# One transformer layer on one core: unit 1's keys moved behind unit 0's scores, w_out's first half made in two steps, and the first pair's sums issued in the second pair

## The chip, the cores and the metric

The kernel runs on one core of a Trainium2 chip. Its time is the device time of one execution in microseconds (us). The engines of the core work side by side, each through its own list of instructions and in that list's order: TensorE (PE; its weight loads are shown as PEld), VectorE (DVE), ScalarE (ACT), GpSimd (POOL) and SyncE (SP), from which nearly all DMA transfers are issued. An instruction that waits holds up all that stands behind it on its engine.

## The reference

The reference computes one layer over 1024 latent tokens (a grid 64 wide) and 256 context tokens, model width 1024, all in fp32. Cut to what matters here:

```
h = modulate(rms_norm(x)); one projection gives q, k, v of two mixers A and B
o_a = windowed grouped-query attention      (8 heads of 64, context keys in the same softmax)
o_b = 2-D neighbourhood attention           (8 heads; 640 keys for 128 queries: 384 latent, 256 context)
x   = x + g1 * (concat(rms_norm(o_a), rms_norm(o_b)) @ w_out)      # 1024 x 1024
h2  = modulate(rms_norm(x))
out = x + g2 * ((silu(h2 @ w_gate) * (h2 @ w_up)) @ w_down)        # hidden width 2816
```

## The kernel before, in words

**Precision.** Products are made from fp32 operands split in two: `hi` is the operand rounded to a shorter format (a copy on ACT or a cast on DVE, L117 or L119), and `lo` is what is left (a subtraction on DVE or POOL, L120). A product is three matmuls: hi by hi, hi by lo, lo by hi. Line 120 is thus the line of very many instructions, and the tile's name tells which.

**Order.** The program is written in an order of its own, but the framework puts each engine's list in the order in which its own timeline has the instructions ready, with the written order as the tie's end. `tc.issue_after(ins)` asks that what is issued inside stands behind `ins` in that timeline. So moving a call in the source can move rows on every engine.

**Attention B and the output projection (about 430 to 700 us).** Mixer B is done in 16 units u = (C, hp_): C one of four column blocks, hp_ one of four pairs of heads. For a pair of heads `b_kv` loads the keys in four pieces (`kkb`, L557), transposes them on PE (L562) and copies them as fp32r into `KTb` (DVE L567, one piece in four by ACT L565). `b_q` does the like for queries (`qdb`, L574, L579; `QThb`, `QTlb`). `b_front` computes scores `s` into PSUM (L458, four for a unit), takes them with the bias `bt` off on DVE (`P`, `nm`, L620), puts them through the exponential on ACT (L622), and at the end takes the reciprocal of the sums (DVE L626) and scales four tiles `P` on POOL (L628). `b_back` transposes `P` (L642, copied to `PT` at L645 and L647), and multiplies with the values (L655 to L659). In the loop over u the front of one unit runs woven with the back of the unit before.

In the same loop the half of the output projection that takes mixer A's rows runs for u = 2 to 8 (`out_a`): `w_out`'s four tiles of 128 rows (`woraw`) are loaded in two halves each (L793, L794), scaled by a column on POOL (L799) and split into `wo`, hi on ACT, lo on POOL for the first and third tile and on DVE for the second and fourth (L120). All of this is `load_wo(0)`, called once at u = 1. `in_a` loads a block of mixer A's output (`oal`, L831), `out_proj` splits it on DVE (`oh` L119, `ol` L120) and multiplies (L823 to L825).

**FFN (about 700 to 1160 us).** The hidden width is done in 11 pairs jp of 256. For each pair `group(jp)` does the gate half and then the up half. Each half is a two-by-two block product made from seven products of sums (numbered 1 to 7), 12 matmuls each. Products 1, 5, 7 and 6 go to new banks of PSUM. Product 5 is copied out by ACT (`p5`, L1114), 7 and 6 are added on DVE to `p5` and `p1` (L1116, L1118). Then product 2 is accumulated onto bank 1, product 3 onto bank 5 and product 4 onto bank 7. For the first three pairs products 1 and 2 were made before. In the gate half DVE adds `p1` to the banks (`sg`, L1128, L1129), POOL adds the two (L1130), ACT takes SiLU (L1132). In the up half DVE adds (`uc`, L1141), POOL multiplies (L1137, L1138, L1142). The right operands are `B11`, `BT1`, `BT3`, `BT2`, `B22`, `BT4` for the products 1, 5, 7, 6, 3, 4. The weights of a half are loaded (`fraw`, L993), combined on POOL (`fs`, L980) and split into `fwhl` one half ahead. `f_combs(jp, gate)` then makes four sums of the pair's four gated tiles on DVE (`sc`, L1089 to L1092) for the third product (`w_down`), and three of the gated tiles and the four sums are stored to the array `f_d` in DRAM. From the third pair on pieces of a modulation (`gw`, L1053, DVE L1055) are put in between.

**w_down (about 1160 us to the end)** reads `f_d` back and multiplies, again in sums.

Of the kernel before, what the change touches and what calls it, by code (L numbers as in the profile page):

```python
# [43 lines left out]
US, UR = 13, 13  # L44
# [17 lines left out]
def block(tc, d, out, dbg=()):  # L62
# [386 lines left out]
    at = pool("at", bufs=2)  # L449

    def scores(segs, lh, ll):
        s = psA.tile([128, 1024], F32, name="s", tag="s", bufs=2)
        for n_, l in enumerate((lh, ll)):
            for o, rhs, n in segs:
                ov = s[:, o:o + n]
                if len(rhs.shape) == 3:
                    ov = ov.rearrange("p (r c) -> p r c", c=rhs.shape[2])
                T.matmul(ov, l, rhs, start=n_ == 0, stop=n_ == 1)  # L458
        return s
# [88 lines left out]

    kvs, vps = {}, {}

    def b_kv(hp_):
# [49 lines left out]
    def b_front(hp_, C, Ps, QT, bias):  # L601
# [4 lines left out]
        for R in range(2):  # L606
            r0 = 4 * R
            for h in range(2):
# [7 lines left out]
                else:  # L616
# [4 lines left out]
                                       3.0e38, ALU.add, ALU.min, nm[:, j:j + 1])  # L621
                S.activation(P, P, AF.Exp, scale=-1.0, bias=nm[:, j:j + 1],  # L622
                             accum_out=den[:, j:j + 1])
                Ps.append(P)
                yield
        V.reciprocal(den, den)  # L626
        for j in range(4):
            G.tensor_scalar(Ps[j], Ps[j], den[:, j:j + 1], 1.0, ALU.mult, ALU.mult)  # L628

# [93 lines left out]
    for u in range(16):  # L723
# [30 lines left out]
        if u == UR + 1:  # L754
            qtb[0] = b_q(0, 0)
            kin = {0: b_kin(0, 0)}
        if u == UR + 2:
            b_kv(1)
    qtb[1] = b_q(1, 0)
    PsB = []  # L760
    stores_done()
    run(b_front(0, 0, PsB, qtb[0], kin[0][0]), prev)
    o_rstd(0)
    at.release()
# [23 lines left out]
    def load_wo(grp):  # L788
        ws = []
        for c in range(4):  # L790
            raw = op.tile([128, D], F32, name="woraw", tag="xt", bufs=xtb[0])
            if grp == 0:
                load(raw[0:64], d["w_out"][c * 64:c * 64 + 64])  # L793
                load(raw[64:128], d["w_out"][256 + c * 64:256 + c * 64 + 64])  # L794
            else:
                load(raw, d["w_out"][512 + c * 128:512 + (c + 1) * 128])
            r = col[:, 64 + 4 * grp + c:65 + 4 * grp + c]
            if c in WOG:
                G.tensor_scalar(raw, raw, r, 1.0, ALU.mult, ALU.mult)  # L799
            else:  # L800
                V.tensor_scalar(raw, raw, r, None, ALU.mult)
            hl = wop.tile([128, 2, D], F32R, name="wo", bufs=4)
            split(hl[:, 0], hl[:, 1], raw, S, V if c % 2 else G)
            ws.append(hl)
        return ws
# [92 lines left out]
    for u in range(16):  # L898
# [16 lines left out]
        if 1 <= u < 9:  # L915
            if u == 1:
                wo = load_wo(0)
                nxt = in_a(0)
            else:
                out_a(u - 2, *nxt)  # L920
            if u == 8:
                out_a(7, *in_a(7))
                wo = load_wo(1)
        elif 9 <= u < 15:
# [160 lines left out]
    def f_combs(jp, gate):  # L1085
# [6 lines left out]
        V.tensor_tensor(s[3], a12, s[1], op=ALU.subtract)  # L1092
        return [(f_d[n - 1, jp], x) for n, x in
                ((1, a11), (2, a12), (4, a22), (5, s[0]), (6, s[1]), (7, s[2]), (3, s[3]))]

    def group(jp, early=None):
        gate = []
        for which, w in enumerate(FW):
# [4 lines left out]
            for n in (1, 5, 7, 6):  # L1103
# [13 lines left out]
                else:  # L1117
                    V.tensor_tensor(p1, pb[6], p1, op=ALU.add)  # L1118
            u2, v = p1, p5
# [14 lines left out]
            else:  # L1134
# [4 lines left out]
                for n, o in ((5, 1), (7, 2)):  # L1139
                    c = ev("uc")  # L1140
                    V.tensor_tensor(c, pb[n], u2, op=ALU.add)  # L1141
                    last[0] = G.tensor_tensor(gate[o], c, gate[o], op=ALU.mult)  # L1142
        return f_combs(jp, gate)[1 if early else 0:]

# [77 lines left out]

    ops1 = operands(1)
    for jp in range(NJ // 2):
        made = group(jp, early[jp] if jp < NA else None)
        if jp == NJ // 2 - 1:
# [187 lines left out]
```

## Time and profile before

| | |
|---|---|
| median of 3 runs | 1366.87 us (1366.67 to 1369.6) |
| profiled execution | 1369.69 us, its span 1367.6 us |
| mean granted TensorE clock | 0.987 |
| PE | 1299.4 us busy, 95% of the span |
| DVE | 920.5 us, 67% |
| ACT | 595.3 us, 44% |
| POOL | 620.0 us, 45% |

Times in the profile are us from the span's start. A row of a timeline gives start, length, engine, line of the kernel, operation, what is written and read, and in brackets the idle time of that engine just before it with the event that ended it. The granted clock is given as a share of full speed: 1.00 is 2.4 GHz, 0.50 is 1.2 GHz.

### The profile page before, as it was taken

The page shows a single profiled execution, that of the slowest core. Times are in us where ns is not written, and L with a number is a line of the kernel's source. Part 1 is how long each engine was busy: PE and PEld are TensorE (multiplying, and loading weights), DVE is VectorE, ACT ScalarE, POOL GpSimd, SP SyncE. Part 2 cuts the span into 40 slices and gives each one's busy share as a digit, 9 for nine tenths or more (in the row PEclk, how much of TensorE's full clock was granted, in tenths as well). Part 3 has the DMA queues.
Part 4 walks back from the last instruction along what each step waited for, and adds up shares of the span by engine and source line. Part 5 has one row for each costly group of instructions (what it writes and reads, how often), then busy time and mean ns, then how long its engine had stood idle before and what let it go on. Part 6 is the DMA issues. An engine that isn't in the chain of part 4 may idle for free. (4 is left out here: it accounts for less than half of the span.)

```text
span 1367.6 us, 18930 instructions
## 1 busy us (share of the span) xinstructions
PE 1299.4 (95%) x6537; PEld 1014.9 (74%) x6537; DVE 920.5 (67%) x1536; ACT 595.3 (44%) x1201; POOL 620.0 (45%) x537
## 2 busy tenths in 40 slices
PE   6998998999998799999979989999999999999997
PEld 4677886767666577777757768887887887888886
DVE  5687775577546564566567788757868776858662
ACT  5555424554455544455555423333332333654430
POOL 1477665342113444575414777677687663000000
PEclk9999999999999999999999999999999999999999
DMA  9445374265227766555273344455565554985732
GB/s 349 156 145 195 101 192 101 65 197 185 93 87 233 220 211 205 183 192 178 95 215 95 98 155 157 167 189 185 186 233 177 190 185 165 393 296 212 258 101 61
DMA packets 149571, 242.85 MB, mean 178 GB/s; under 512 B 43932, under 2 KB 66660, under 8 KB 149348
## 3 DMA queue, kind: packets, MB, share of 16 engines
q1 hardware_dynamic: 149476, 241.65, 53.8%
q8 instruction: 51, 0.84, 0.3%
q14 instruction: 44, 0.36, 0.1%
HBM read 177.91 MB, written 63.70 MB: 177 GB/s over the span
## 5 line engine op out<-in xcount | busy, mean ns | idle before, releaser
L1241 PE MATMUL pf<-dhl 128*128 128x512 f32 x588 | 134.9, 389 | 0.0
L256 PE MATMUL pg<-whi,hl 128*128 128x512 f32 (+1 forms) x368 | 133.0, 375 | 0.5 <-POOL hl L120 0.5
L254 PE MATMUL pg<-whi,hTh 128*128 128x512 f32 (+1 forms) x320 | 122.3, 382 | 7.5 <-ACT qc L329 5.7
L1241 PEld LDWEIGHTS pf<-dhl 128*128 128x128 f32 x588 | 110.4, 188 | 22.9
L255 PE MATMUL pg<-wlo,hTh 128*128 128x512 f32 (+1 forms) x320 | 120.8, 377 | 0.0
L120 DVE TENSOR_TENSOR fwhl<-fs,fwhl 128x512 fp32r<-128x512 f32 x88 | 96.6, 1106 | 31.1 <-ACT fwhl L117 15.5
L500 POOL TENSOR_SCALAR P<-P,den 128x640 f32<-128x640 f32 (+1 forms) x64 | 51.8, 828 | 118.4 <-DVE den L498 84.0
L980 POOL TENSOR_TENSOR fs<-fraw 128x512 f32<-128x512 f32 x44 | 62.9, 1436 | 85.7 <-DMA fraw<-in_w_up_dram 52.1
L256 PEld LDWEIGHTS pg<-whi,hl 128*128 128x128 f32 x368 | 70.5, 192 | 12.3 <-issue 0.8
L1241 PE MATMUL pf<-fdhl 128*128 128x512 f32 x336 | 78.4, 390 | 0.5 <-DVE fdhl L120 0.4
L120 DVE TENSOR_TENSOR dhl<-draw,dhl 128x512 fp32r<-128x512 f32 x98 | 62.6, 686 | 24.1 <-ACT dhl L117 24.1
L117 ACT ACTIVATE dhl<-draw 128x512 fp32r<-128x512 f32 x98 | 55.8, 624 | 51.3 <-PE pf L1241 42.5
L254 PEld LDWEIGHTS pg<-whi,hTh 128*128 128x128 f32 x320 | 61.6, 192 | 20.3 <-ACT qc L329 7.2
L117 ACT ACTIVATE fwhl<-fs 128x512 fp32r<-128x512 f32 x88 | 54.8, 627 | 48.9 <-PE pf L1019 41.6
L1241 PEld LDWEIGHTS pf<-fdhl 128*128 128x128 f32 x336 | 62.9, 188 | 14.4 <-DVE fdhl L120 1.4
L117 ACT ACTIVATE fwhl<-fraw 128x512 fp32r<-128x512 f32 x54 | 34.0, 630 | 80.8 <-PE pf L1019 72.8
L490 ACT ACTIVATE P<-P,nm 128x640 f32<-128x640 f32 (+1 forms) x64 | 51.0, 798 | 40.3 <-DVE nm L488 40.2
L255 PEld LDWEIGHTS pg<-wlo,hTh 128*128 128x128 f32 x320 | 61.8, 193 | 8.8
L120 DVE TENSOR_TENSOR fwhl<-fraw,fwhl 128x512 fp32r<-128x512 f32 x54 | 68.2, 1262 | 0.1
L628 POOL TENSOR_SCALAR P<-P,den 128x640 f32<-128x640 f32 x64 | 50.8, 815 | 34.8 <-DVE den L626 28.2
L488 DVE CUSTOM_DVE_ANT_0 P<-s,mska,nsink 128x640 f32<-128x640 f32 (+1 forms) x64 | 52.4, 846 | 18.1 <-PE s L458 15.9
L622 ACT ACTIVATE P<-P,nm 128x640 f32<-128x640 f32 x64 | 52.7, 824 | 16.4 <-DVE nm L620 16.4
(315 smaller groups left out, 3583.6 us busy)
## 6 DMA issues: line engine op xcount, KB each, us to landing
draw<-f_d SPq DMA_DIRECT2D x35, 512.0 KB
bt<-in_bias_b_dram SPq DMA_DIRECT2D x16, 1024.0 KB
wraw<-in_w_mod_dram SPq DMA_DIRECT2D x48, 256.0 KB
fraw<-in_w_gate_dram SPq DMA_DIRECT2D x22, 512.0 KB
fraw<-in_w_up_dram SPq DMA_DIRECT2D x22, 512.0 KB
wr<-in_w_down_dram SPq DMA_DIRECT2D x22, 512.0 KB
f_d<-sc SPq DMA_DIRECT2D x44, 256.0 KB
t_d<-wt SPq DMA_DIRECT2D x44, 256.0 KB
```

Source lines behind the costliest of these rows:

```text
L117: S.activation(hi, src, AF.Copy)
L120: lo_eng.tensor_tensor(lo, src, f(hi), op=ALU.subtract)
L254: T.matmul(pg[:, :n], l, w[0][:, :n], start=k == 0, stop=False)
L255: T.matmul(pg[:, :n], l, w[1][:, :n], start=False, stop=False)
L256: T.matmul(pg[:, :n], hl[m // 4, k][:, m % 4 * 128:m % 4 * 128 + 128], w[0][:, :n], start=False, stop=k == 7)
L488: V.tensor_tensor_reduce(P[:, :n], s[:, s0:s0 + n], mska[:, m0:m0 + n], -1.0, nsink[:, hh:hh + 1], ALU.add, ALU.min, nm[:, h:h + 1])
L490: S.activation(P[:, :n], P[:, :n], AF.Exp, scale=-1.0, bias=nm[:, h:h + 1], accum_out=den[:, h:h + 1])
L500: G.tensor_scalar(Ps[h][:, :n], Ps[h][:, :n], den[:, h:h + 1], 1.0, ALU.mult, ALU.mult)
L622: S.activation(P, P, AF.Exp, scale=-1.0, bias=nm[:, j:j + 1], accum_out=den[:, j:j + 1])
L628: G.tensor_scalar(Ps[j], Ps[j], den[:, j:j + 1], 1.0, ALU.mult, ALU.mult)
L980: G.tensor_tensor(t, x, y, op=op_)
L1241: T.matmul(pd[t], a[:, x, l], b[:, y], start=start and i == 0, stop=stop and i == 2, skip_group_check=True)
```

## The change

Three edits. The unit's numbers count from 0.

1. `b_kv(1)`, the keys of the second pair of heads, was called in mixer A's loop. It is now called after `b_front(0, ...)`, and asked to stand behind the last score matmul of unit 0 (`scored[0]`).
2. `load_wo` only loads the four tiles of `w_out`; scaling and splitting are in `make_wo`. At u = 1 the loads and `in_a(0)` are called. At u = 2 `make_wo(0)` and `out_a(0)` are called, behind the last exponential, the reciprocal and the last scaling on POOL of unit 2 (the third unit).
3. For pair 0 `group` stores only the gated tiles. The four sums of this pair and their four stores are called in the gate half of pair 1 and asked to stand behind the addition of product 6 onto `p1` (L1118 before). For all other pairs nothing changes but the place in the text.

```diff
@@ scores
-                T.matmul(ov, l, rhs, start=n_ == 0, stop=n_ == 1)
+                scored[0] = T.matmul(ov, l, rhs, start=n_ == 0, stop=n_ == 1)
...
+    @contextmanager
+    def behind(after):
+        with ExitStack() as st:
+            for x in after:
+                st.enter_context(tc.issue_after(x.ins))
+            yield
...
@@ b_front
-        V.reciprocal(den, den)
+        marks[:] = [ex, V.reciprocal(den, den)]
         for j in range(4):
-            G.tensor_scalar(Ps[j], Ps[j], den[:, j:j + 1], 1.0, ALU.mult, ALU.mult)
+            sc = G.tensor_scalar(Ps[j], Ps[j], den[:, j:j + 1], 1.0, ALU.mult, ALU.mult)
+        marks.append(sc)
...
-        if u == UR + 2:
-            b_kv(1)
...
     run(b_front(0, 0, PsB, qtb[0], kin[0][0]), prev)
+    with tc.issue_after(scored[0].ins):
+        b_kv(1)
...
             if u == 1:
-                wo = load_wo(0)
+                raws = load_wo(0)
                 nxt = in_a(0)
+            elif u == 2:
+                with behind(marks):
+                    wo = make_wo(0, raws)
+                    out_a(0, *nxt)
             else:
                 out_a(u - 2, *nxt)
...
@@ group
-                    V.tensor_tensor(p1, pb[6], p1, op=ALU.add)
+                    taken = V.tensor_tensor(p1, pb[6], p1, op=ALU.add)
+            if which == 0 and between:
+                with tc.issue_after(taken.ins):
+                    between()
...
-        return f_combs(jp, gate)[1 if early else 0:]
+        if jp:
+            return made + f_combs(jp, gate)
+        kept.append(gate)
+        return made
...
+    def first_sums():
+        for x in f_combs(0, kept[0]):
+            load(*x)
...
-        made = group(jp, early[jp] if jp < NA else None)
+        made = group(jp, early[jp] if jp < NA else None, first_sums if jp == 1 else None)
```

The number of instructions of each kind is the same on every engine. Their order differs in two places, at about 430 to 505 us and about 776 to 815 us. Lines move by up to 40 numbers: L620 becomes L633, L628 becomes L641, L799 becomes L821, L1089 to L1092 become L1115 to L1118, L1116 becomes L1141, L1118 becomes L1143, and L120 becomes L121.

The first place is VectorE while the second and third units of mixer B are at work. Numbers behind a name tell buffers apart: `KTb21` holds the keys of the second head of pair 2, and `oh`, `ol` are made from `oal`, the block that `in_a(0)` loads. Before:

```order
L567 CAST KTb21_4897<-pt_4906 128x128
L567 CAST KTb21_4897<-pt_4911 128x512
L119 CAST oh_5111<-oal_4955 128x512
L620 ISA P_4978,nm_4971<-s_4973,bt_4920 128x640
L620 ISA nm_4971 128x1
L567 CAST KTb21_4897<-pt_4917 128x128
L120 TENSOR_TENSOR ol_5112<-oal_4955,oh_5111 128x512
L120 TENSOR_TENSOR wo_4938<-woraw_4934,wo_4938 128x1024
L620 ISA P_4996,nm_4971<-s_4991,bt_4920 128x640
```

Of the change, from the last cast of `KTb21` on:

```order
L580 CAST KTb21_4897<-pt_4917 128x128
L633 ISA P_4980,nm_4955<-s_4975,bt_4920 128x640
L633 ISA nm_4955 128x1
L659 COPY PT_4984<-pt_4983 128x512
L633 ISA P_4997,nm_4955<-s_4992,bt_4920 128x640
L633 ISA nm_4955 128x1
L633 ISA P_5014,nm_4955<-s_5009,bt_4920 128x640
L633 ISA nm_4955 128x1
L121 TENSOR_TENSOR QTlb_4952<-pt_4946,QThb_4951 128x512
L659 COPY PT_5018<-pt_5017 128x512
L639 RECIPROCAL den_4956<-den_4956 128x4
L120 CAST oh_5111<-oal_4939 128x512
```

The cast `oh` and the subtraction `ol` moved from the middle of the casts of `KTb21` to behind the reciprocal of the third unit, and the casts of `KTb30`, `KTb31` follow them there.

The second place is GpSimd, over the same stretch. Before, from the scaling of the second unit's tiles on:

```order
L628 TENSOR_SCALAR P<-P,den 128x640 x4
L799 TENSOR_SCALAR woraw<-woraw,col 128x1024 x4
L120 TENSOR_TENSOR wo<-woraw,wo 128x1024 x2
L628 TENSOR_SCALAR P<-P,den 128x640 x4
L670 TENSOR_TENSOR sr<-sr,osq 128x256
```

Of the change, with the second and third units' scalings in one row:

```order
L641 TENSOR_SCALAR P<-P,den 128x640 x8
L821 TENSOR_SCALAR woraw<-woraw,col 128x1024 x4
L684 TENSOR_TENSOR sr<-sr,osq 128x256
L121 TENSOR_TENSOR wo<-woraw,wo 128x1024 x2
L641 TENSOR_SCALAR P<-P,den 128x640 x4
```

The scaling and splitting of `w_out` stood ahead of the third unit's four tiles `P`; they stand behind them now, and ahead of the fourth unit's.

The third place is VectorE in the gate half of the second FFN pair. `p5_8020` (`p5_8008` in the change) is that half's `p5`, `sg_7...` are tiles of the first pair, `fwhl` weights of the coming half. Before:

```order
L120 TENSOR_TENSOR fwhl_8099<-fs_8097,fwhl_8099 128x512
L1089 TENSOR_TENSOR sc_7966<-sg_7855,sg_7857 128x512
L1090 TENSOR_TENSOR sc_7967<-sc_7966,sg_7455 128x512
L1091 TENSOR_TENSOR sc_7968<-sg_7455,sg_7855 128x512
L120 TENSOR_TENSOR fwhl_8104<-fs_8102,fwhl_8104 128x512
L1092 TENSOR_TENSOR sc_7969<-sg_7856,sc_7967 128x512
L1116 TENSOR_TENSOR p5_8020<-pf_8022,p5_8020 128x512
L120 TENSOR_TENSOR fwhl_8107<-fraw_8085,fwhl_8107 128x512
L1118 TENSOR_TENSOR p1_7555<-pf_8036,p1_7555 128x512
L120 TENSOR_TENSOR fwhl_8205<-fs_8203,fwhl_8205 128x512
L1128 TENSOR_TENSOR sg_8074<-pf_8007,p1_7555 128x512
```

Of the change:

```order
L121 TENSOR_TENSOR fwhl_8099<-fs_8097,fwhl_8099 128x512
L121 TENSOR_TENSOR fwhl_8104<-fs_8102,fwhl_8104 128x512
L1141 TENSOR_TENSOR p5_8008<-pf_8010,p5_8008 128x512
L121 TENSOR_TENSOR fwhl_8107<-fraw_8085,fwhl_8107 128x512
L1143 TENSOR_TENSOR p1_7555<-pf_8024,p1_7555 128x512
L1115 TENSOR_TENSOR sc_8038<-sg_7855,sg_7857 128x512
L121 TENSOR_TENSOR fwhl_8205<-fs_8203,fwhl_8205 128x512
L1116 TENSOR_TENSOR sc_8039<-sc_8038,sg_7455 128x512
L1117 TENSOR_TENSOR sc_8040<-sg_7455,sg_7855 128x512
L1118 TENSOR_TENSOR sc_8041<-sg_7856,sc_8039 128x512
L1156 TENSOR_TENSOR sg_8074<-pf_7995,p1_7555 128x512
```

The four sums moved from ahead of the two additions that take product 7 and product 6 out of PSUM to behind them, and they now stand ahead of the addition L1128 (L1156) for `sg`.

## Rows read from the trace of the kernel before

**Rows 1.** The page: span, and each engine's busy time

```profile
span 1367.6 us, 18930 instructions
...
PE 1299.4 (95%) x6537; PEld 1014.9 (74%) x6537; DVE 920.5 (67%) x1536; ACT 595.3 (44%) x1201; POOL 620.0 (45%) x537
```

**Rows 2.** Stretches: length; PE, PEld, DVE, ACT, POOL busy; clock, DMA share, GB/s

```profile
430.00:505.00 75.00, 63.82 (x389) 45.58 (x388) 43.33 (x86) 36.11 (x73) 32.01 (x32) 0.93 0.72 223
466.00:471.00 5.00, 0.46 (x2) 0.46 (x3) 2.50 (x5) 2.35 (x4) 3.97 (x3) 0.71 1.12 314
505.00:700.00 195.00, 190.87 (x1191) 143.76 (x1190) 118.35 (x239) 98.47 (x215) 100.08 (x106) 1.00 0.55 171
793.50:799.30 5.80, 5.75 (x14) 4.52 (x15) 3.47 (x6) 0.79 (x2) 0.62 (x2) 0.51 0.81 271
800.00:1160.00 360.00, 356.76 (x1565) 292.77 (x1563) 265.42 (x272) 117.75 (x203) 246.66 (x162) 1.00 0.53 178
1160.00:1367.60 207.60, 200.69 (x884) 165.89 (x884) 132.89 (x214) 86.59 (x154) 0.00 (x0) 1.00 0.63 222
```

**Rows 3.** PE's waits, 430 to 505 us: us, count, longest

```profile
PE s L458 <- DVE KTb L567: 4.9, 1, 4.9
```

**Rows 4.** PE's timeline in the attention stretch: start, length, instruction, idle before

```profile
470.54 0.90 PE L458 MATMUL s<-KTb,QThb 128*128 128x256 f32 x2 [4.89 <-DVE KTb L567]
...
480.35 0.66 PE L562 MATMUL pt<-ident,kkb 128*128 128x128 f32 x4 [0.75 <-ACT PT L647]
...
503.07 0.66 PE L659 MATMUL pO<-PT,vp 128*64 128x128 f32 x8
```

**Rows 5.** VectorE's timeline in the same stretch

```profile
468.50 1.06 DVE L119 CAST oh<-oal 128x512 fp32r<-128x512 f32 x1 [4.19 <-DMA oal<-oa_d]
...
472.24 3.38 DVE L120 TENSOR_TENSOR wo<-woraw,wo 128x1024 fp32r<-128x1024 f32 x1
```

**Rows 6.** GpSimd's timeline in the same stretch

```profile
468.15 1.12 POOL L799 TENSOR_SCALAR woraw<-woraw,col 128x1024 f32<-128x1024 f32 x1 [0.86 <-DMA woraw<-in_w_out_dram]
469.24 5.29 POOL L120 TENSOR_TENSOR wo<-woraw,wo 128x1024 fp32r<-128x1024 f32 x2
...
481.49 3.13 POOL L628 TENSOR_SCALAR P<-P,den 128x640 f32<-128x640 f32 x4 [6.96 <-DVE den L626]
```

**Rows 7.** SyncE's queue in the same stretch, DMA issues

```profile
460.59 0.33 SPq L831 DMA_DIRECT2D oal<-oa_d  x1
...
464.85 3.73 SPq L557 DMA_DIRECT2D kkb<-kb_d  x2
```

**Rows 8.** PE's timeline in the second FFN pair

```profile
787.51 0.39 PE L1016 MATMUL pf<-BT1h,fwhl 128*128 128x512 f32 x1
793.55 0.79 PE L1016 MATMUL pf<-BT4h,fwhl 128*128 128x512 f32 x1 [5.65 <-DVE p L1116]
...
809.68 0.39 PE L1016 MATMUL pf<-BT4h,fwhl 128*128 128x512 f32 x1
...
812.40 0.39 PE L1016 MATMUL pf<-BT1h,fwhl 128*128 128x512 f32 x1
```

**Rows 9.** VectorE's timeline in the second FFN pair

```profile
785.52 1.76 DVE L1089 TENSOR_TENSOR sc<-sg 128x512 f32<-128x512 f32 x1 [1.19 <-POOL sg L1138]
787.31 1.65 DVE L1090 TENSOR_TENSOR sc<-sc,sg 128x512 f32<-128x512 f32 x1
788.89 1.75 DVE L1091 TENSOR_TENSOR sc<-sg 128x512 f32<-128x512 f32 x1
790.56 1.74 DVE L120 TENSOR_TENSOR fwhl<-fs,fwhl 128x512 fp32r<-128x512 f32 x1
792.22 0.68 DVE L1092 TENSOR_TENSOR sc<-sg,sc 128x512 f32<-128x512 f32 x1
792.83 0.68 DVE L1116 TENSOR_TENSOR p<-pf,p 128x512 f32<-128x512 f32 x1
```

**Rows 10.** GpSimd's timeline in the second FFN pair

```profile
799.20 1.30 POOL L980 TENSOR_TENSOR fs<-fraw 128x512 f32<-128x512 f32 x1 [5.18 <-DMA fraw<-in_w_up_dram]
```

More of the change, by code (lines that the diff above doesn't have):

```diff
@@ L3 @@
 from concourse import mybir
+from contextlib import ExitStack, contextmanager
 from itertools import chain
@@ L449, in block @@
     at = pool("at", bufs=2)
+    scored = [None]
     def scores(segs, lh, ll):
@@ L549, in block @@
     kvs, vps = {}, {}
+    marks = []
+    @contextmanager
[4 more added lines that the diff above has]
+            yield
     def b_kv(hp_):
@@ L621, in b_front @@
                                        3.0e38, ALU.add, ALU.min, nm[:, j:j + 1])
-                S.activation(P, P, AF.Exp, scale=-1.0, bias=nm[:, j:j + 1],
-                             accum_out=den[:, j:j + 1])
+                ex = S.activation(P, P, AF.Exp, scale=-1.0, bias=nm[:, j:j + 1],
+                                  accum_out=den[:, j:j + 1])
                 Ps.append(P)
                 yield
-        V.reciprocal(den, den)
+        marks[:] = [ex, V.reciprocal(den, den)]
         for j in range(4):
-            G.tensor_scalar(Ps[j], Ps[j], den[:, j:j + 1], 1.0, ALU.mult, ALU.mult)
+            sc = G.tensor_scalar(Ps[j], Ps[j], den[:, j:j + 1], 1.0, ALU.mult, ALU.mult)
+        marks.append(sc)
     def b_back(hp_, C, Ps, vp):
@@ L788, in load_wo @@
     def load_wo(grp):
-        ws = []
+        raws = []
         for c in range(4):
@@ L796, in load_wo, with make_wo @@
                 load(raw, d["w_out"][512 + c * 128:512 + (c + 1) * 128])
+            raws.append(raw)
+        return raws
+    def make_wo(grp, raws):
+        ws = []
+        for c, raw in enumerate(raws):
             r = col[:, 64 + 4 * grp + c:65 + 4 * grp + c]
@@ L922, in block @@
                 out_a(7, *in_a(7))
-                wo = load_wo(1)
+                wo = make_wo(1, load_wo(1))
         elif 9 <= u < 15:
@@ L1092, in f_combs, with group @@
         V.tensor_tensor(s[3], a12, s[1], op=ALU.subtract)
-        return [(f_d[n - 1, jp], x) for n, x in
-                ((1, a11), (2, a12), (4, a22), (5, s[0]), (6, s[1]), (7, s[2]), (3, s[3]))]
-    def group(jp, early=None):
+        return [(f_d[n - 1, jp], x) for n, x in ((5, s[0]), (6, s[1]), (7, s[2]), (3, s[3]))]
+    def group(jp, early=None, between=None):
         gate = []
@@ L1142, in group @@
                     last[0] = G.tensor_tensor(gate[o], c, gate[o], op=ALU.mult)
-        return f_combs(jp, gate)[1 if early else 0:]
+        a11, _, a12, a22 = gate
+        made = [(f_d[n - 1, jp], x) for n, x in ((1, a11), (2, a12), (4, a22))][1 if early else 0:]
+        if jp:
+            return made + f_combs(jp, gate)
+        kept.append(gate)
+        return made
     early = []
@@ L1223, in block @@
     ops1 = operands(1)
+    kept = []
+    def first_sums():
+        for x in f_combs(0, kept[0]):
+            load(*x)
     for jp in range(NJ // 2):
-        made = group(jp, early[jp] if jp < NA else None)
+        made = group(jp, early[jp] if jp < NA else None, first_sums if jp == 1 else None)
         if jp == NJ // 2 - 1:
```

## The prediction

> **What bounds the kernel now.** The page says that PE is busy for 95% of the span [rows 1], so time is to be had only where PE stands still or runs slowly. I therefore read the stretches next, to see which stages have such places. From 505 to 700 us PE is busy 98%, from 800 to 1160 us 99%, in the last stage 97%, all at clock 1.00 [rows 2]: there a gain on another engine is worth nothing, but also what is gained ahead of them is carried to the end unshortened, since PE sets the pace behind it. The 75 us of the attention stretch are otherwise: 63.82 us busy, so 11.2 us idle, at a mean clock of 0.93 [rows 2]. A clock of 0.93 for 75 us is a deficit of 5.25 us of full speed. Of that 0.29 x 5 = 1.45 us fell into 466 to 471 us, where PE had next to nothing to do [rows 2], so 3.8 us cost time. Lost in this stretch: 11.2 + 3.8 = 15.0 us. In the second FFN pair PE's timeline shows a hole of 5.65 us and behind it matmuls at a clock of 0.51 [rows 2, 8]. Its loss is measured from the rows: from the start at 787.51 to that at 812.40 are 24.89 us for 72 matmuls; twelve matmuls at full speed take 812.40 - 809.68 = 2.72 us [rows 8], 72 take 16.3; lost 8.5 us (8.57). The two places together lose 23.5 us, and they are where the change's order differs.
>
> The waits and then VectorE's and GpSimd's timelines tell who holds PE. In attention the largest wait is 4.9 us for a cast of `KTb` on DVE [rows 3]. DVE had not been slow: it stood at the cast `oh`, in its list ahead of that cast, and waited 4.19 us for `oal` [rows 5], which SP had issued at 460.59 [rows 7]. In the FFN PE waits for L1116, which frees the bank; DVE came to it at 792.83 because three sums, a split of weights and the fourth sum stood in front [rows 9].
>
> **Part 1, keys behind scores, and w_out behind the third softmax.** They work on the same stretch, so I price them together, by laying the new order's rows one behind another with the durations of before, each starting when its engine is free and its operands are there.
>
> What goes: `oh` and `ol` leave the casts of `KTb21`, so the hole of 4.89 us before 470.54 [rows 4] has no cause left. On GpSimd the third unit's four scalings no longer stand behind four scalings of `w_out` (1.12 each), two splits (5.29) and the small row behind: 4 x 1.12 + 5.29 = 9.8 us of work [rows 6]. They took 3.13 us from 481.49 on, and were held by `den` of that unit for 6.96 us [rows 6], so that this order costs nothing by itself before, and gains only if `den` comes earlier now; it does, by what PE's scores gain.
>
> What comes or stays, in the laid-out order: (a) casts of `KTb30` stand behind `oh` and `ol`: 0.7 us of PE waiting; (b) those of `KTb31` likewise 1.05; (c) the fourth unit's scores need a buffer whose reader stands on DVE behind a `wo` split of 3.38 us [rows 5], and wait 2.75; (d) small waits (for `nm` and `PT`) about 1.0; (e) slow clock behind these, about 1.5, an estimate from the 3.8 of before and holes that are half as long. Together 7.0 us of the 15.0 stay, and 8.0 go.
>
> The keys of the fourth unit are an operation whose landing the trace of before doesn't show at the new place. On SP they stand behind eight halves of `w_out`, `oal`, a bias and queries, and I get their issue at 456 to 460 and PE's need at 466.5 to 470. The nearest row is `oal`: issued at 460.59, its reader started at 468.50, so 7.9 us, with the DMA engines full (a share of 1.12 in that stretch) [rows 2, 5, 7]. By that row they land at 464 to 468, in time or 1 to 2 us late for the first. Before, the last pair was issued by 468.6 (464.85 + 3.73) and first used at 480.35, where PE's wait was not for them [rows 4, 7]; by this row 12 us are enough but less isn't shown. I take 1.0 us late, so a gain of 7.0. Bounds: only 2 of the 15 stay, a gain of 13; or the DMA is late by as much as is gained and more, a loss (below).
>
> Of the rest, marks and the stores are without price: the same instructions, and the projection `out_a(0)` moves as a block of 24 matmuls that PE executes either way.
>
> **Part 2, the first pair's sums.** In the new order L1116 stands behind two splits `fwhl` and no sum. The first ends where the sums began, before 785.52; the second takes 1.74 [rows 9] beside GpSimd, then the addition 0.68: finished near 787.3, or 786.8 if the split is shorter. PE needs it at about 787.7, one matmul after 787.51 [rows 8]. So the hole of 5.65 goes, and with it the slow stretch behind it: 5.8 us at 0.51 [rows 2] is about 2.8 us of time. Together 8.5.
>
> What is late next: the sums now stand between L1118 and L1128. The four sums are 1.76 + 1.65 + 1.75 + 0.68 = 5.84 us [rows 9], and L1128, with all that DVE does for the up half, comes later by that against PE. Also PE, being earlier, meets the weights' load: the up half's next `fraw` let GpSimd start only at 799.20, after 5.18 us of waiting [rows 10], on a DMA that doesn't come earlier because PE does. Laid out, PE does the gate's product 4 to 790.2 and the up half's products 5, 7, 6 to 798.4; product 3 then must wait for `p5` of that half, which ACT gives behind a SiLU that waits for GpSimd's L1130, itself behind the `fs` of 799.20. I get 800.4, a new wait of 2.0 us, and 0.5 us of slower clock behind it. Gain 8.5 - 2.5 = 6.0. Bounds: nothing new, 8.5; the chain as late as today's 799.20 row and with L1130 behind two such rows, 3; and 0 if L1116 is late again.
>
> The row pairs bear on how fast DVE gets through. A subtraction of 512 elements between two tiles in SBUF took 1.65 to 1.76 us at three places and 0.68 at the fourth [rows 9]. The Trainium skill (SBUF — State Buffer, "🔬 SBUF: two separate sides") says that DVE and GpSimd share a pair of ports as an exclusive lock: a two-input DVE operation and a GpSimd operation that reads SBUF exclude each other for a whole instruction. By it the moved sums are as dear at the new place if GpSimd is at work there, and would be 4 x 0.68 = 2.7 us if it stands waiting as before 799.20. The rows fit it, and it speaks against the change: a late sum may also stop the GpSimd work that gives L1130.
>
> On the clock: behind the hole of 5.65 us PE's granted clock was 0.51, so its lower level of 1.2 GHz, and it was 1.00 again from 800 on [rows 2, 8]. The Trainium skill (TensorE: Matmul & The Clock Gate, "What's actually happening") says that the throttled state is the default and activity releases it. By it the slow stretch goes with the hole; if it stayed the gain of part 2 would be 2.8 less.
>
> **Sum.** -7.0 - 6.0 = -13.0 us. Against the profiled execution's own 1369.69 this is 1356.7. The median of the runs is 1366.87, 2.8 lower; the same gain from there is 1353.9, and I predict 1354.
>
> **The rivals.**
>
> A: attention gains nothing, PE's idle time only moves. For it: `w_out`'s 9.8 us on GpSimd now stand directly ahead of the fourth unit's scalings, and 3.38 us of DVE splits ahead of its casts [rows 5, 6], so the same wait may come one unit later. Against it: `oal` has landed by then, so that the 4.19 us of pure DMA waiting on DVE have no successor. Time 1366.87 - 6 = 1361; 1364 if part 2 gives its low bound of 3.
>
> B: both holes close well: only 2 us stay in attention and nothing new comes in the FFN, 13 + 8.5 = 21.5: 1345. For it: the large wait has one cause [rows 3]. Against it: DVE is still in one list with GpSimd at its side.
>
> C: part 2 gives nothing. `p5` has only 0.4 us to spare at 787.7, and the weights' chain [rows 10] is late for the up half: the hole moves from product 4 to product 3. Then only attention's 7.0: 1360.
>
> D, slower: the keys of the fourth unit land late. PE's list has their transposes ahead of the scores and of the projection, so each us late is a us of PE standing. The mechanism is the DMA engines' queue: eight halves of `w_out` (256 KB each) and a bias stand before them in a stretch that moves 314 GB/s [rows 2]. Each us costs 1 us and the slow clock behind a hole adds a fifth to a half, as in the FFN 8.5 for 5.65. From 10 us past PE's need (480, as late as before) the 13 us of the whole change are gone; 14 us give about 1372. The rows of `oal` speak against it (7.9 us under full load).
>
> That the change does nothing is excluded by the order: both lists differ at just the waiting rows.
>
> **How the numbers follow.** Both gains as summed 0.53 (own range 1349 to 1359), A 0.16, B 0.10, C 0.09, D 0.12. What a measurement of this kernel can tell from no change is 0.2%, 2.7 us: 1364.1 to 1369.6. Faster: 0.53, all of B, 0.10 of A, 0.07 of C: 0.80. Within: 0.06 of A, 0.02 of C, 0.02 of D: 0.10. Slower: the other 0.10 of D. The range leaves out D's slower part and a little at the low end: 1344 to 1366.
>
> **What would show it.** In attention: no wait of PE for `KTb` above 2 us, `oh` without idle time before it, the third unit's scalings ahead of `w_out`'s first on GpSimd with less than 3 us of waiting, PE's busy share of the corresponding 67 us at 94% or more. In the FFN: L1141 (L1116 before) ends before 788, no hole ahead of `BT4`, a wait of about 2 us ahead of the up half's `B22` with `p5` or `fraw` as its cause, and clock 1.00 over the pair. From there to the end everything is shifted by the same amount. Wrong would be: a wait for a `kkb` of over 3 us (D), `KTb` or `P` waits in the fourth unit that add up to over 10 us (A), a hole of over 5 us in the up half (C).

## The result

The changed kernel is faster by two thirds of a per cent: 1359.48 us median (1354.71 to 1364.57) against 1367.93 us (1364.32 to 1371.47), 8 runs each, ratio 0.9934, 95% interval 0.9915 to 0.9952. Run once more beside later kernels it had 0.9946 (0.9928 to 0.9964). The forecast was 13 us less; it became some 9 (9.0 by the ratio, 8.5 by the medians). The profiled execution took 1358.09 us, span 1356.3.

The spans of the two profiles differ by 11.3 us. To see where, I take PE's own marks from its timelines: the start of the fourth unit's last value matmuls (the row of eight, 517.44 before and 511.30 after), of the first BT1 matmul of pair 1's gate half (776.63 and 766.66), and of pair 3's (842.32 and 831.89). That gives four stretches:

| stretch | before | after | less |
|---|---|---|---|
| start to the fourth unit's last value matmuls | 517.44 | 511.30 | 6.14 |
| from there to pair 1 (rest of attention, projection, pair 0) | 259.19 | 255.36 | 3.83 |
| pairs 1 and 2 | 65.69 | 65.23 | 0.46 |
| pair 3 to the end of the span | 525.28 | 524.41 | 0.87 |

So attention gave what was forecast, the FFN pair nearly nothing, and a stretch for which nothing was forecast gave something. The page of the changed kernel, answering to [rows 1]:

```profile
span 1356.3 us, 18923 instructions
...
PE 1296.4 (96%) x6537; PEld 1012.8 (75%) x6537; DVE 917.8 (68%) x1536; ACT 594.4 (44%) x1201; POOL 620.6 (46%) x537
```

**Attention.** The same view of stretches as [rows 2], first of after:

```profile
430.00:505.00 75.00, 68.55 (x436) 50.05 (x434) 45.91 (x97) 39.50 (x80) 35.71 (x35) 0.95 0.82 236
441.00:453.00 12.00, 11.76 (x88) 9.27 (x87) 8.52 (x20) 6.92 (x14) 2.82 (x3) 1.00 1.03 264
468.85:474.90 6.05, 6.05 (x31) 4.28 (x31) 1.31 (x4) 1.56 (x4) 5.65 (x6) 0.53 0.95 269
```

and one stretch of before that the prediction had not looked at:

```profile
441.00:453.00 12.00, 12.00 (x65) 7.76 (x64) 4.30 (x8) 4.68 (x10) 2.79 (x4) 0.87 0.49 158
```

The last three numbers are PE's clock, the DMA engines' share and GB/s. From 441 to 453 us the clock was 0.87 before and 1.00 after, the DMA share 0.49 before and 1.03 after. SyncE's queue shows what goes with the second. Before, it stood for 10 us at queries before it came to `w_out`:

```profile
441.78 10.23 SPq L574 DMA_DIRECT2D qdb<-qb_d  x3
...
454.54 0.55 SPq L793 DMA_DIRECT2D woraw<-in_w_out_dram  x1
```

After, with unit 1's keys behind unit 0's scores, the same load is issued 9 us earlier, `oal` 6.6 us earlier than in [rows 7], and the fourth unit's first `kkb` at 459.59:

```profile
445.42 0.57 SPq L808 DMA_DIRECT2D woraw<-in_w_out_dram  x1
...
454.02 0.34 SPq L853 DMA_DIRECT2D oal<-oa_d  x1
...
459.59 0.36 SPq L570 DMA_DIRECT2D kkb<-kb_d  x1
```

PE's waits in the stretch, answering to [rows 3], and the longest of them in PE's timeline with the mark that answers to the fourth unit:

```profile
PE pt L575 <- DMA kkb<-kb_d: 3.2, 1, 3.2
PE s L461 <- DVE KTb L580: 1.4, 2, 1.1
PE s L461 <- DVE nm L633: 1.0, 1, 1.0
```

```profile
468.85 1.09 PE L575 MATMUL pt<-ident,kkb 128*128 128x128 f32 x4 [3.17 <-DMA kkb<-kb_d]
...
511.30 0.66 PE L673 MATMUL pO<-PT,vp 128*64 128x128 f32 x8
```

The wait of 4.89 us for `KTb` is gone; the largest is now for the fourth unit's keys, 9.3 us after their issue, and the 6 us behind it ran at a clock of 0.53.

**FFN.** VectorE's addition of product 7 ends at 777.3, before PE needs it, as forecast. But PE has a hole of 5.15 us one half later, ahead of product 3 (`B22`) of the up half. PE, ACT, VectorE and GpSimd there:

```profile
794.23 0.79 PE L1042 MATMUL pf<-B22h,fwhl 128*128 128x512 f32 x1 [5.15 <-ACT p L1139]
```

```profile
792.54 1.15 ACT L1160 ACTIVATE sg<-sg 128x512 f32<-128x512 f32 x2 [4.92 <-DVE sg L1157]
793.60 0.58 ACT L1139 ACTIVATE p<-pf 128x512 f32<-128x512 f32 x1
```

```profile
776.65 0.68 DVE L1141 TENSOR_TENSOR p<-pf,p 128x512 f32<-128x512 f32 x1
...
791.31 0.60 DVE L1081 TENSOR_SCALAR acc<-gw,sil 128x512 f32<-128x512 f32 x1 [4.28 <-DMA gw<-in_w_mod_dram]
791.83 0.68 DVE L1157 TENSOR_TENSOR sg<-pf,p 128x512 f32<-128x512 f32 x1
```

```profile
789.15 1.26 POOL L1006 TENSOR_TENSOR fs<-fraw 128x512 f32<-128x512 f32 x1 [4.46 <-DMA fraw<-in_w_up_dram]
790.36 1.26 POOL L1158 TENSOR_TENSOR sg<-p,p 128x512 f32<-128x512 f32 x1
```

The copy of `p5` (L1139) stands on ACT directly behind two SiLU. One waits for VectorE's addition L1157, which stands behind a piece of the modulation whose DMA is late; the other for GpSimd's L1158, behind a combination whose weights are late.

### The profile page after: what moved, and what is told of

Its sections match the earlier page's. It is cut to its first block, busy times and chain, and to the rows that moved or that the text cites. A ratio compares the mean times of both kernels' runs of the same rounds, so it can differ in the third digit from the quotient of the medians.

```text
span 1356.3 us, 18923 instructions
## 1 busy us (share of the span) xinstructions
PE 1296.4 (96%) x6537; PEld 1012.8 (75%) x6537; DVE 917.8 (68%) x1536; ACT 594.4 (44%) x1201; POOL 620.6 (46%) x537
## 5 line engine op out<-in xcount | busy, mean ns | idle before, releaser
L121 DVE TENSOR_TENSOR fwhl<-fs,fwhl 128x512 fp32r<-128x512 f32 x88 | 95.7, 1096 | 29.2 <-ACT fwhl L118 21.7
L121 DVE TENSOR_TENSOR dhl<-draw,dhl 128x512 fp32r<-128x512 f32 x98 | 62.4, 684 | 24.2 <-ACT dhl L118 24.2
L121 DVE TENSOR_TENSOR fwhl<-fraw,fwhl 128x512 fp32r<-128x512 f32 x54 | 69.2, 1281 | 0.1
L641 POOL TENSOR_SCALAR P<-P,den 128x640 f32<-128x640 f32 x64 | 51.3, 822 | 37.0 <-DVE den L639 34.8
L491 DVE CUSTOM_DVE_ANT_0 P<-s,mska,nsink 128x640 f32<-128x640 f32 (+1 forms) x64 | 52.4, 846 | 18.4 <-PE s L461 16.1
L849 POOL TENSOR_TENSOR xa<-xa,xt 128x512 f32<-128x512 f32 x28 | 40.9, 1460 | 38.7 <-DVE xa L848 24.8
```

Source lines behind the costliest of these rows:

```text
L121: lo_eng.tensor_tensor(lo, src, f(hi), op=ALU.subtract)
L491: V.tensor_tensor_reduce(P[:, :n], s[:, s0:s0 + n], mska[:, m0:m0 + n], -1.0, nsink[:, hh:hh + 1], ALU.add, ALU.min, nm[:, h:h + 1])
L641: sc = G.tensor_scalar(Ps[j], Ps[j], den[:, j:j + 1], 1.0, ALU.mult, ALU.mult)
L849: added[0] = add.tensor_tensor(dst[:, cs], dst[:, cs], base[:, cs], op=ALU.add)
```

## The experiments

All ratios are to the kernel before, run beside them. The three stretches are taken from each run's PE timeline as above, so they are those of one execution of each. The rest of the span, pair 3 to the end, was 521.2 to 523.5 us, mean 521.9, in the six runs that have a modulation half a pair later (those with `gw` in their name), and 522.3 to 525.5, mean 524.1, in the six others and the changed kernel.

| kernel | median us | ratio (95%) | to 4th unit | to pair 1 | pairs 1, 2 |
|---|---|---|---|---|---|
| attn_only | 1359.69 | 0.9930 (0.9916 to 0.9943) | 509.05 | 257.16 | 66.27 |
| ffn_only | 1367.88 | 0.9985 (0.9974 to 0.9995) | 516.63 | 259.03 | 65.20 |
| silu_behind_p5 | 1358.58 | 0.9916 (0.9902 to 0.9930) | 512.34 | 257.49 | 63.60 |
| gw_later | 1356.64 | 0.9906 (0.9890 to 0.9922) | 507.92 | 257.24 | 65.58 |
| without_kv | 1367.05 | 0.9979 (0.9966 to 0.9992) | 518.65 | 258.36 | 65.06 |
| without_wo | 1364.12 | 0.9960 (0.9945 to 0.9976) | 511.67 | 257.81 | 64.82 |
| silu_and_gw | 1355.64 | 0.9889 (0.9862 to 0.9916) | 509.50 | 256.99 | 58.95 |
| silu_gw_kkb5 | 1359.30 | 0.9919 (0.9899 to 0.9939) | 511.84 | 258.63 | 58.78 |
| after_again | 1361.12 | 0.9946 (0.9928 to 0.9964) | 510.92 | 258.11 | 65.60 |
| silu_and_gw_2 | 1356.68 | 0.9912 (0.9892 to 0.9932) | 507.64 | 257.76 | 65.26 |
| silu_and_gw_no_sums | 1356.55 | 0.9911 (0.9891 to 0.9931) | 509.11 | 257.63 | 66.20 |
| silu_gw_wo_late | 1364.61 | 0.9975 (0.9959 to 0.9992) | 521.81 | 255.69 | 63.21 |

**attn_only**, the sums' edit undone:

```diff
...
-        made = group(jp, early[jp] if jp < NA else None, first_sums if jp == 1 else None)
+        made = group(jp, early[jp] if jp < NA else None, None)
```

> The changed kernel with the third edit undone (the first pair's sums stand where they stood); attention edits kept. Theory 1 (attention gave 7 us, the sums about 1 us, because the hole in the second pair only moved; what else differs between the two profiles, 3.8 us at 690 to 716 us, is a DMA's landing and no part of the change): 7 us below before, ratio 0.995, and the hole of 5 to 6 us before product 4 of the gate half is there as in the kernel before. Theory 2 (the attention gain is partly given back before the FFN, and the sums give the 6 us that were predicted): 3 us below before, ratio 0.998.

Measured 0.9930, as much as the whole change gave. PE's waits from 775 us on show the old hole:

```profile
PE pf L1042 <- DVE p L1141: 8.1, 5, 5.8
```

**ffn_only**, the attention edits undone:

```diff
+        if u == UR + 2:
+            b_kv(1)
...
-    with tc.issue_after(scored[0].ins):
-        b_kv(1)
...
-                raws = load_wo(0)
+                wo = make_wo(0, load_wo(0))
...
```

> The kernel before with the third edit alone (sums of the first pair behind the additions of products 7 and 6). Theory 1 (the hole moves from product 4 of the gate half to product 3 of the up half): 1 us below before, ratio 0.999, a hole of about 5 us before B22 of the up half, ended by ACT's p. Theory 2 (sums are worth what was predicted): 6 us below, ratio 0.996.

Measured 0.9985 (0.9974 to 0.9995), 2 us, and pairs 1 and 2 shorter by 0.5 us. The wait is there again, for ACT's copy:

```profile
PE pf L1038 <- ACT p L1135: 4.9, 1, 4.9
```

**gw_later** and **silu_behind_p5** take the two things in front of that copy apart. gw_later:

```diff
-            if jp >= GS:
+            if jp >= GS and (jp, which) != (GS, 0):
                 next(g2_steps, None)
```

> The changed kernel, and the first piece of the modulation (gw, acc2) comes half a pair later, so VectorE's second addition for sg no longer stands behind its DMA. Theory 1 (the SiLU that waits longest is that of GpSimd's addition, behind the weight load, which this leaves as it is): p5 about 0.8 us earlier, 1 us below the changed kernel, ratio to before 0.993. Rival (the modulation's DMA wait of 4.28 us on VectorE is the cause of the hole): 4 to 6 us below the changed kernel, ratio 0.989 to 0.990.

The modulation is not the cause: with its piece later L1157 comes early (785.44), and the hole is 5.01 us all the same, with GpSimd's addition as what ACT waits for.

```profile
792.56 0.79 PE L1042 MATMUL pf<-B22h,fwhl 128*128 128x512 f32 x1 [5.01 <-ACT p L1139]
```

```profile
791.39 0.63 ACT L1160 ACTIVATE sg<-sg 128x512 f32<-128x512 f32 x1 [4.61 <-POOL sg L1158]
791.93 0.58 ACT L1139 ACTIVATE p<-pf 128x512 f32<-128x512 f32 x1
```

The run's time is lower than the changed kernel's, but not by these pairs. The edit moves every piece of the modulation by half a pair, and from pair 3 on PE then waits less for VectorE's additions. Its waits from 775 us on in the changed kernel and in gw_later:

```profile
PE pf L1042 <- DVE p L1141: 2.0, 3, 0.8
```

```profile
PE pf L1042 <- DVE p L1141: 0.5, 1, 0.5
```

The rest of the span goes with these waits in the other runs too: 1.8 us or more of them and 524.3 us or more in before, the changed kernel, attn_only, silu_behind_p5, without_wo and after_again, at most 0.5 us and 522.0 us or less in five of the six with the modulation later; the three that are left lie between.

silu_behind_p5:

```diff
-                    S.activation(p5, pb[5], AF.Copy)
+                    held = S.activation(p5, pb[5], AF.Copy)
+                    if which and jp == 1:
+                        with tc.issue_after(held.ins):
+                            for x in gate[1:]:
+                                S.activation(x, x, AF.Silu)
...
-                for x in s[1:]:
+                for x in s[1:] if jp != 1 else ():
```

> The changed kernel, and in the second pair the three SiLU of the gate half are issued behind the copy of the up half's p5 on ACT instead of ahead of it. Theory 1 (the new hole of 5.15 us in the up half is there because that copy stands in ACT's list behind two SiLU, whose inputs wait for GpSimd's addition behind a weight load and for VectorE's piece of the modulation): the copy comes at about 787 instead of 793.6, the hole goes and with it the slow clock behind it, 5 to 7 us below the changed kernel, ratio to before about 0.989. Rival (the up half is held by the weights' load as such, so the hole moves to the next product): not more than 1.5 us below the changed kernel, ratio about 0.993.

The hole ahead of `B22` is gone, so the copy's place was its cause. But two others came, ahead of product 4 of the up half and of pair 2's gate half, and pairs 1 and 2 gained 1.6 us, not 5 to 7:

```profile
797.35 0.50 PE L1042 MATMUL pf<-BT4h,fwhl 128*128 128x512 f32 x1 [2.83 <-DVE p L1145]
814.26 0.50 PE L1042 MATMUL pf<-BT4h,fwhl 128*128 128x512 f32 x1 [3.02 <-DVE p L1145]
```

**silu_and_gw** has both edits.

> The changed kernel with both: the second pair's SiLU behind the up half's p5, and the first piece of the modulation half a pair later. Theory 1 (with p5's copy free, VectorE's additions behind the modulation's DMA are what is late next, as the holes of 2.83 and 3.02 us in silu_behind_p5 showed): the first of these holes goes, the second gets smaller; pairs 1 and 2 together take 61 to 62 us, against 65.2 of the changed kernel; 3 to 4 us below the changed kernel, ratio to before about 0.9895. Rival (the weights' load and its combinations on GpSimd set the pace of these two pairs, whatever is reordered): the holes come back at the next product, pairs 1 and 2 together 63.5 us or more, ratio 0.992.

Pairs 1 and 2 took 58.95 us, 6.3 less than in the changed kernel, with one hole of 1.53 us left. But the profiled execution, 1348.92 us, is one of two that stand apart: the six took 1347.52, 1348.92 and 1355.32 to 1360.53 us. Repeated as **silu_and_gw_2** it did not stay so.

> silu_and_gw once more. Theory 1 (the sums' edit is worth what was forecast once p5's copy and the additions are free): pairs 1 and 2 together near 59 us, as in the first run (58.95) against 65.2 of the changed kernel; 5 to 6 us below after_again. Rival (its fast executions were the start or the end of the program, not these pairs): pairs as said, but the time is within 3 us of after_again.

Pair 1 again ran without a hole, but in pair 2 PE waited 5 us for VectorE, and the pairs took 65.26 us:

```profile
808.89 0.79 PE L1042 MATMUL pf<-BT4h,fwhl 128*128 128x512 f32 x1 [5.00 <-DVE p L1145]
```

The stretch before that hole, columns as in [rows 2]:

```profile
800.00:810.00 10.00, 5.00 (x21) 3.80 (x20) 10.00 (x10) 1.26 (x2) 7.66 (x5) 0.88 0.38 143
```

VectorE is busy for all 10 us. Two rows of GpSimd, the last combination of one half's weights and that two halves later, stand at 779.07 and 805.75 in silu_and_gw, at 781.54 and 808.38 in silu_and_gw_2: 26.7 and 26.8 us. So the work of GpSimd and VectorE runs through these pairs at the same pace in both, and only its start against PE differs: 12.6 us behind the start of pair 1 in the one (766.49), 16.1 in the other (765.40).

That difference arises in pair 0. First silu_and_gw, then silu_and_gw_2: one combination of GpSimd, and the load of the next weights that SyncE issues right behind it:

```profile
742.28 1.58 POOL L1006 TENSOR_TENSOR fs<-fs,fraw 128x512 f32<-128x512 f32 x1 [4.30 <-DVE fwhl L121]
743.90 0.33 SPq L1019 DMA_DIRECT2D fraw<-in_w_up_dram  x1
```

```profile
741.20 13.06 POOL L1006 TENSOR_TENSOR fs<-fs,fraw 128x512 f32<-128x512 f32 x1 [4.30 <-DVE fwhl L121]
754.28 0.33 SPq L1019 DMA_DIRECT2D fraw<-in_w_up_dram  x1
```

VectorE is busy without a gap from 740 to 755 us in both. In silu_and_gw GpSimd's row gets in between, and the row of VectorE beside it (L1209) takes 1.75 us; in silu_and_gw_2 that one takes 0.68, and GpSimd's row lasts until 754.26. It lasts 13.05 or 13.06 us in twelve of the fourteen profiled executions, the kernels before and after among them, and 1.58 in two, silu_and_gw and silu_gw_kkb5, which are the two with pairs 1 and 2 below 60 us. What lets GpSimd in first is not known, and no edit tried it.

**silu_and_gw_no_sums** undoes the sums' edit under both.

> silu_and_gw with the third edit undone: the sums of the first pair stand ahead of the additions of products 7 and 6 again. Theory 1 (the sums' edit and the two later ones work only together): the hole of 5 to 6 us before product 4 of the second pair's gate half is back, pair 1 takes 35 to 36 us, and the time is 5 to 7 us above silu_and_gw_2. Rival (the new holes were the matter, and the sums could have stayed): no hole over 2.5 us there, time within 2 us of silu_and_gw_2.

The hole came back as theory 1 said, 5.83 us ahead of the gate's product 4, and pair 2 had none. But the time is that of silu_and_gw_2, as the rival said, though not for its reason: there the same 5 us stood in pair 2.

```profile
784.20 0.80 PE L1042 MATMUL pf<-BT4h,fwhl 128*128 128x512 f32 x1 [5.83 <-DVE p L1145]
```

**without_kv** and **without_wo** undo one attention edit each, by the lines shown for ffn_only.

> The changed kernel with the first edit undone (unit 1's keys stand ahead of unit 0's scores again). Theory 1 (the wait for KTb goes by the second edit, w_out behind the third softmax, and the keys' edit only fills smaller holes near 435 to 440 us): no wait of PE for KTb over 2 us, 5 to 7 us below before, ratio 0.995 to 0.996. Rival (both are needed, one without the other moves the wait): not more than 2 us below before, ratio 0.9985 or more.

The largest `KTb` wait is 1.0 us, as theory 1 said, but the gain is not there: the fourth unit's last value matmuls start at 518.65, later than before. (The time, 0.9979, lies between the two theories.) The fourth unit's keys are waited for instead:

```profile
477.09 0.74 PE L575 MATMUL pt<-ident,kkb 128*128 128x128 f32 x5 [2.57 <-DMA kkb<-kb_d]
478.57 1.05 PE L575 MATMUL pt<-ident,kkb 128*128 128x128 f32 x4 [0.74 <-DMA kkb<-kb_d]
...
488.85 0.56 PE L461 MATMUL s<-KTb,QThb 128*128 128x256 f32 x2 [1.81 <-DVE nm L633]
```

> The changed kernel with the second edit undone (w_out's first half is scaled and split, and the first block of mixer A's output is cast, at u = 1 again). In the order of VectorE the cast oh then stands ahead of all casts of the third unit's keys. Theory 1: PE waits for a KTb cast behind oh's DMA by 5 us or more, as before, and the time is that of ffn_only, 0 to 2 us below before, ratio 0.9985 to 1.000. Rival (the keys' edit alone does most of it, since it brings the loads into order): 4 us or more below before, ratio 0.997 or less.

Here the rival was right on the time (0.9960) though theory 1 was right on the order. VectorE still stands at `oh` for its DMA, and PE for a cast behind it, but that DMA was issued at 451.81, 8.8 us earlier than in [rows 7], and so was its end (459.73 against 468.50):

```profile
459.73 1.17 DVE L120 CAST oh<-oal 128x512 fp32r<-128x512 f32 x1 [3.04 <-DMA oal<-oa_d]
```

```profile
461.15 1.11 PE L575 MATMUL pt<-ident,kkb 128*128 128x128 f32 x4 [4.09 <-DVE KTb L580]
```

**silu_gw_kkb5** and **silu_gw_wo_late** try to mend the new wait for `kkb`, the one with `KKB = 5` for 4, the other with the third and fourth tile of `w_out` loaded later:

```diff
...
+                with tc.issue_after(kload[0].ins):
+                    for c in (2, 3):
+                        load_a(c, raws[c])
                 with behind(marks):
```

> As silu_and_gw, and a fifth buffer for kkb, so that the first piece of the fourth unit's keys is issued ahead of w_out's loads. Theory 1 (PE's wait of 3.2 us for kkb and the slow clock behind it come from that piece's place in the DMA queue): the wait is under 1 us or moves to the second piece with at most 2 us, 1 to 4 us below silu_and_gw, ratio about 0.988. Rival (the DMA engines are full from 440 to 468 us, so another piece is late by as much): the wait stays at 2.5 us or more in sum and the time is that of silu_and_gw.

The first piece was no longer waited for, the second was, and the scores behind it; the fourth unit ended no earlier (511.84). (Its profiled execution, 1352.66 us, is the fastest of the six by 3.9 us.)

```profile
468.74 0.74 PE L575 MATMUL pt<-ident,kkb 128*128 128x128 f32 x5 [1.71 <-DMA kkb<-kb_d]
...
482.01 0.56 PE L461 MATMUL s<-KTb,QThb 128*128 128x256 f32 x2 [2.04 <-DVE nm L633]
```

> silu_and_gw, and the third and fourth tile of w_out's first half are loaded behind the fourth unit's keys instead of ahead of them. Theory 1 (the keys are late because 2 MB of w_out stand before them in full DMA engines): PE's wait of 2.5 to 3.2 us for kkb goes, together with the slow clock behind it; the projection's matmuls come later and fill other places; the fourth unit's back ends 2 to 5 us earlier. Rival (the DMA engines are full as a whole, and what is put off is waited for elsewhere): a wait for w_out's tiles or for their splits takes its place, and the fourth unit's back ends within 1.5 us of silu_and_gw_2.

PE's wait for `kkb` stayed at 2.06 us. The fourth tile's load went behind values and further queries in SyncE's queue (481.06), and the projection waited for its split; the fourth unit ended 14 us later than in silu_and_gw_2. So the rival was right that what is put off is waited for elsewhere, but the price was far larger than the 1.5 us that it named.

```profile
494.40 1.22 PE L849 MATMUL pg<-wo,oh 128*128 128x512 f32 x2 [5.09 <-ACT wo L118]
```

**after_again**, the changed kernel beside the last three:

> The changed kernel once more, beside the following three on one chip. All theories: 8 to 10 us below before, ratio 0.993 to 0.9945, with the hole of 5 us before product 3 of the second pair's up half.

It came as expected, with the hole of 5.18 us ahead of `B22`. Against it silu_and_gw_2 is 4.4 us faster by the medians; the intervals overlap a little, but all six executions of the one (1353.71 to 1359.84) lie below all five of the other (1360.81 to 1362.83). So a version faster than both kernels was run (0.9889 and 0.9912). gw_later and silu_and_gw_no_sums are as fast within their intervals, and what these have in common is the modulation half a pair later, with its shorter rest of the span. silu_behind_p5 is nearly as fast without it (0.9916), so the times alone don't settle it.

## Why the prediction was right or wrong

**The time** was within the range and the sign right; 13 us were forecast, 9 came. One of the two terms held, the other failed, and a gain that no term had made up for part of it.

**Attention, 7.0 forecast.** Right in size. Over the eight runs with both attention edits and no other change there the fourth unit's mark lies at 507.6 to 512.3, mean 509.7; in the two without either at 517.0. That is 7.3 us. (The eight are up to 6 us apart already at unit 0's first scores; counted from there it is 80.5 against 87.8 us, 7.3 again.) That the sum fits is partly luck. The new wait for `kkb` was in it with 1 us and was 3.2 (1.7 to 4.2 in the others), over the 3 us named as the sign of rival D, and the slow clock behind it, 0.47 x 6.05 us, cost 2.8 where 1.5 was laid out for the whole stretch. Against that the wait of 2.75 us for the scores' buffer came as 1.0 (`nm`). The step that named the cause was only half right. It gave the gain to the second edit, since `oh` leaves the casts. The runs show that this edit alone moves the wait to the next keys (518.65), and that the first alone gives 5.4 of the 7.3 (517.0 - 511.67; one run). What it does had been in no term. In that run PE still waits 4.09 us for `KTb`; what is gone stood earlier. Before, PE waited for unit 1's own keys:

```profile
438.93 0.74 PE L562 MATMUL pt<-ident,kkb 128*128 128x128 f32 x5 [1.71 <-DMA kkb<-kb_d]
```

Behind that wait it ran at 0.87 from 441 to 453 us, which is 0.13 x 12 = 1.6 us, and waited 1.06 us for queries (`QTlb`) at 454.59. None of the three, 4.3 us in sum, is in without_wo or in the changed kernel; without_kv has all three again. The first edit also lets SyncE get to the loads while the DMA engines were half idle: the share of 441 to 453 us is 1.00 in without_wo and 0.49 in without_kv, and `w_out` and `oal` are issued 6 to 9 us earlier. How much of the gain comes from that, no run separates. I had read who waits for `oal`, and the DMA share only over the whole stretch and at 466 to 471 us, where it was full anyway.

**FFN, 6.0 forecast, 0.5 measured** in pairs 1 and 2. The first half of the step held: L1141 early, no hole ahead of `BT4`. The term that failed is the new wait, laid out at 2.0 plus 0.5 us. It was 5.15 us, and 7.7 us from 794.2 on ran at 0.70:

```profile
794.20:801.90 7.70, 7.67 (x24) 6.16 (x25) 5.55 (x7) 2.16 (x4) 5.71 (x4) 0.70 0.53 170
```

The wait and 0.30 x 7.7 us are 7.5 of the 8.5 us removed, and small waits took half a us more. This is rival C's case, with its hole at the product that it named and nearly its time of 1360 us; the cause it gave, the weights' chain, was right too. (Its time fits better than its gain, 7.0 against 8.5 to 9.0: it started from a median of before that was 1.1 us lower than that of all eight runs.) The weights themselves came as laid out: GpSimd's row `fs` started 22.6 us behind the start of pair 1 before (799.20 - 776.63) and 22.5 us after (789.15 - 766.66). Mis-sized was the chain behind it. From that row to product 3 at 800.4 the layout left 1.2 us, which is less than the row itself takes (1.30 in [rows 10]). In the changed kernel GpSimd's addition (1.26 us), two SiLU (1.15) and the copy of `p5` (0.58) stand behind it, and ACT waited 0.9 us longer for VectorE's L1157: 5.03 us from 789.15 to the end of the copy at 794.18. So the gain fell below even the 3 us laid out as the low bound for a late chain. The experiments say more: whichever instruction is freed, PE runs until it meets the next thing that GpSimd or VectorE gives it. It met it at the gate's product 4 (before, attn_only, no_sums), the up half's product 3 (changed kernel, gw_later, ffn_only), or pair 2 (silu_and_gw_2), at about 5 us each. So in these two pairs the pace is theirs, by the rows of silu_and_gw and its repetition. Only in two executions (silu_and_gw and silu_gw_kkb5) did they start 3.5 us earlier against PE, and the holes shrank to 1.5 us and less: those where the one row of GpSimd in pair 0 took 1.58 us and not 13.06. That row had been in no term.

**"Carried to the end unshortened"** held only from pair 3 on, and there the sentence before it failed: a gain on another engine was not worth nothing, since the modulation half a pair later took 2.2 us off that rest (524.1 - 521.9). Between the fourth unit and pair 1 the eight runs took 255.4 to 258.1 us, mean 257.2, against 259.1 without the attention edits: 2 us more gain. PE's wait for the first weights of the FFN is what differs most, in before and after:

```profile
709.01 0.79 PE L1019 MATMUL pf<-B11h,fwhl 128*128 128x512 f32 x1 [5.58 <-DVE fwhl L120]
```

```profile
701.26 0.50 PE L1045 MATMUL pf<-B11h,fwhl 128*128 128x512 f32 x1 [2.83 <-DVE fwhl L121]
```

In the other runs with both edits that wait was 3.1 to 4.6 us, so part of it is chance. Its cause was not tried. Together 7.3 + 0.5 + 2.0 = 9.8 us, against 9.0 by the ratio (0.0066 x 1367.9) and 8.5 by the medians.

**The two rules weighed.** By the Trainium skill's exclusive lock between VectorE and GpSimd (SBUF — State Buffer, "🔬 SBUF: two separate sides") the moved sums would stay dear beside a working GpSimd. This trace agrees: at the new place they took 1.18, 1.77, 1.78 and 0.68 us, and the one of 0.68 again lay where GpSimd stood waiting. The Trainium skill's rule on the clock (TensorE: Matmul & The Clock Gate, "What's actually happening"), that the throttled state is the default and activity releases it, had the slow clock go with the hole. This trace agrees too, in both directions: it is gone where the old holes were, and the new ones brought it back (0.53 from 468.85 us on, 0.70 from 794.2).

## What to carry to other kernels

Before pricing a moved wait, look also at the smaller waits and the slow clock ahead of it, at the DMA share there and at what the issuing queue stood for: much of the gain of attention lay there. When a hole in the bounding engine is closed, ask which of the other engines' chains will be met next and add up every row of that chain, from the landing of its data to the instruction that frees the bounding engine. Look for what that chain itself was held by earlier: here its start went with one row of 13 us on GpSimd. And undo the edits of a change one by one: in attention one edit alone was worth nothing, and the other most of it.

## What the hardware showed beyond that

The clock can fall behind a wait of only 1.56 us. In the changed kernel, behind such a wait that ended at 684.29, PE ran at 0.50 from 686.2 to 689.6 us; in the kernel before, behind the same wait (690.40 in its timeline), it stayed at 1.00 over the same stretch of the order:

```profile
686.20:689.60 3.40, 3.40 (x9) 2.67 (x8) 3.40 (x7) 1.39 (x3) 0.85 (x1) 0.50 1.06 208
```

```profile
692.30:695.70 3.40, 3.40 (x16) 2.79 (x16) 3.40 (x7) 1.39 (x3) 0.85 (x1) 1.00 1.06 180
```

All fourteen profiled executions have this wait, of 1.56 or 1.57 us. In eight the clock over the same stretch of the order was 0.50 to 0.68, in six 1.00, after_again among them, which is the changed kernel itself. So the same wait costs up to 1.6 us more in some executions (the two rows above have 9 and 16 matmuls, and 7 take 1.6 us at full speed), and the runs don't tell when.
